# Two transformer blocks at 256 positions: the wide and the narrow products of a block in turn instead of in two runs of eight

## The chip, the cores and the metric

The kernel runs on one core of a Trainium2 chip. The metric is the device time of one execution in microseconds (us), as the median of several executions.

## What is computed

Two blocks work on x, 256 positions of 2048 features, all in float32. Each one normalises, mixes, adds, normalises, runs a gated feed-forward network of width 5632 and adds:

```python
x = first_block(x, ...)      # attention (8 differential heads, 8 sparse heads), then FFN
return second_block(x, ...)  # gated linear recurrence over 16 heads, then FFN

h = rms_norm(x, pre_mix_norm[l])
proj = h @ w_in[l]                             # first block: 2048 -> 5656 columns
x = x + rms_norm(mix @ w_out[l], post_mix_norm[l])
h = rms_norm(x, pre_ffn_norm[l])
u = causal_dwconv(h @ w_up[l], conv_w[l], conv_b[l])
gate, up = jnp.split(u, 2, axis=-1)
y = (jax.nn.gelu(gate, approximate=True) * up) @ w_down[l]
x = x + rms_norm(y, post_ffn_norm[l])
```

Nearly all work is in the products with the large weights: `w_in`, `w_out`, `w_up` and `w_down` of both blocks.

## The kernel before

**Split operands.** TensorE multiplies in a reduced float32 format (fp32r). To keep precision, each operand is the sum of a high and a low half in that format, and a product is made as three: weights high by features high, weights high by features low, weights low by features high. ACT makes the high half of a weight unit (`wh`, line 143), DVE the low half (`wl`, line 144), from the raw unit `ws` that SP's queue loads (line 125). A unit is 128 x 1024 values.

**Three kinds of product.** `wave` (lines 399, 400, 406) opens a stage: eight output blocks at once, products of 256 columns. `v_unit` (lines 421, 422, 427) has positions on partitions and weights as the moving operand, up to 512 columns. `block` (lines 359 and 364) is the one that changes. It has features on partitions: its stationary operand is a 128 x 128 piece of the weights and its moving operand is the features of all 256 positions. The feature tile holds high and low halves side by side (`src.pair`), so that one product of 512 columns makes weights-high by both halves, the *wide* product: columns 0 to 255 of the bank collect high by high, columns 256 to 511 high by low. The *narrow* product, 256 columns, adds weights-low by features-high to the second half of the bank. A block adds up 16 pieces of the features, eight from each of two weight units; what one unit serves is called a half-block here: eight wide products with `h`, then eight narrow ones with `l`. `block` is used for 24 blocks of the first block's queries and keys, 56 of the recurrence's gates, and 80 in each feed-forward stage.

**What sets the order.** Instructions are issued in the order in which the program writes them, on each engine for itself. `W.take()` hands out the halves of the current unit, and, before it does, issues the load of a unit four further on and the split of the unit two further on. `ws` has five buffers, `wh` and `wl` three each, so the split of unit i + 2 has to wait until the last product that reads unit i - 1 is done: for `wh` that is the last wide product of the half-block before, for `wl` the last narrow one. Accumulators have four banks named `mm` and some borrowed from the other four, named `bg`.

**Background work.** Everything else (attention heads, the recurrence's heads, evacuation of finished blocks, convolution, gating) is written as generators that the class `Background` holds. `bg.tick()` counts, and every fourth tick calls `step()`, which lets each generator issue its next few instructions. In the stages with heads these contain small matmuls, which go into PE's queue at that place (lines 1237, 1248, 1271 and 1285 for the recurrence). A half-block has eight ticks before the change: behind wide products 0, 1, 3, 4, 6 and 7 and behind narrow products 3 and 7; the stages before it leave the count at a multiple of four, so the steps stand behind the fifth wide product and behind the last narrow one.

Of the kernel before, what the change touches and what calls it, by code (L numbers as in the profile page):

```python
# [170 lines left out]
def two_blocks(ctx: ExitStack, tc: tile.TileContext, a: dict, out: bass.AP, dbg=None):  # L171
    nc = tc.nc
    bg = Background()
# [21 lines left out]
    def mm_ps(*cuts):  # L195

        if not mm_free.free and lend[0] and banks.free:
            t, owner = bg_ps(), banks
        else:
            while not mm_free.free:  # L200
                assert bg.tasks
                bg.step()
            t, owner = ps_mm.tile([P, 512], F32, name="mm"), mm_free
        owner.free -= 1
        if owner is banks:
            lend[0] -= 1
        views = [t[:, a:b] for a, b in cuts]
        left = [len(cuts), owner]
        for v in views:
            mm_use[id(v)] = (v, left)  # L210
        return views
# [133 lines left out]
    def need(src, k):  # L345
        while k not in src.ready:
            assert bg.tasks
            bg.step()

    def block(src):  # L350


        ps, = mm_ps((0, 2 * T))
        for k0 in range(0, KB, 8):
            h, l = W.take()
            for j in range(8):
                k = k0 + j
                need(src, k)
                nc.tensor.matmul(ps, h[:, j, :], src.pair[:, k, :, :], start=k == 0, stop=False)  # L359
                if j % 3 < 2:  # L360
                    bg.tick()
            for j in range(8):
                k = k0 + j
                nc.tensor.matmul(ps[:, T:], l[:, j, :], src.hi[:, k, :], start=False, stop=k == KB - 1)  # L364
                if j % 4 == 3:
                    bg.tick()
        return ps

    def whole(ps):
# [340 lines left out]
    with first:  # L710
# [352 lines left out]
        for i in range(8):  # L1063
            if i % 2 == 0:
                c = slice(i // 2 * CH, (i // 2 + 1) * CH)
                nc.sync.dma_start(x[:, :, c], xv[:, :, c])
            if i in (1, 4, 5):
                c = {1: 1, 4: 2, 5: 3}[i]
                later(evac_v, v_chunk(hhl, VW[c]), c)
            bg.add(start_nsa(i, block(hhl)))  # L1070
            qk = q3.tile([P, 2, T], F32, name="dqk")
            bg.add(start_diff(i, block(hhl), qk, 0))
            bg.add(start_diff(i, block(hhl), qk, 1))
# [362 lines left out]
```

## Time and profile before

| | |
|---|---|
| median of 3 runs | 2579.96 us (2578.93 to 2581.62) |
| the profiled execution | 2579.38 us |
| its span, first to last instruction | 2577.6 us |
| PE (matmul) busy | 2547.7 us, 99% |
| DVE busy | 1771.3 us, 69% |
| ACT busy | 1365.8 us, 53% |
| POOL busy | 46.5 us, 2% |
| mean granted TensorE clock | 0.999 of full speed |

Engines are PE (TensorE's matmuls), PEld (its weight loads, which overlap matmuls), DVE, ACT, POOL and SP. A row of a group of instructions gives line, engine, operation, `out<-in`, shape and count, then busy time in us and the mean duration of one in ns, then idle time before them. A matmul's duration reaches from its start to its modelled end and overlaps with the matmuls behind it, so durations don't add up to time; distances between starts do. A timeline row gives start and length in us of a run of like instructions, with the count at its end. A row on a single line in a short window gives the least, middle and largest duration of the instructions that run in that window, in ns. Blocks run from 103 to 338 us (first block's attention, with other products between), from 485 to 934 (first feed-forward stage), from 1256 to 1722 (recurrence) and from 1875 to 2324 (second feed-forward stage).

### The profile page before, as it was taken

What the parts mean: (1) busy time and instruction counts of PE and PEld (TensorE: products, weight loads), DVE (VectorE), ACT (ScalarE), POOL (GpSimd) and SP (SyncE); (2) the same over time, 40 slices, a digit from 0 to 9 for tenths busy, and PEclk for the clock granted to TensorE, in tenths of its full rate; (3) what the DMA queues carried; (4) which work ended last, traced back from release to release, by engine and by line L of the source; (5) the groups of instructions that cost most, each with busy time, mean ns of one, the idle gap of its engine ahead of it and who ended that gap; (6) DMA issues with size and microseconds to landing.
All of it is one profiled execution on the core that took longest, in us unless ns stands there. A gap on an engine that the chain in (4) does not pass through costs nothing.

```text
span 2577.6 us, 38072 instructions
## 1 busy us (share of the span) xinstructions
PE 2547.7 (99%) x14400; PEld 2223.9 (86%) x14400; DVE 1771.3 (69%) x2967; ACT 1365.8 (53%) x2274; POOL 46.5 (2%) x66
## 2 busy tenths in 40 slices
PE   9999999999999999999999999999999999999998
PEld 9899988988888888889888888888988888888887
DVE  6666655687777764446777777785678877775444
ACT  5655554665555553445555555554565555554443
POOL 0000000000000000000000000000000000000000
PEclk9999999999999999999999999999999999999999
DMA  7854555556555565555544454546556555556554
GB/s 243 263 172 148 170 172 179 173 185 192 189 189 186 192 205 188 188 188 169 165 161 158 142 170 143 166 133 196 166 175 194 189 186 192 190 188 205 188 188 147
DMA packets 134229, 466.13 MB, mean 181 GB/s; under 512 B 15547, under 2 KB 20572, under 8 KB 133532
## 3 DMA queue, kind: packets, MB, share of 16 engines
q1 hardware_dynamic: 130572, 456.11, 54.9%
q10 hardware_dynamic: 2784, 2.92, 0.6%
q0 software_dynamic: 688, 4.65, 0.5%
q8 instruction: 113, 1.85, 0.3%
q14 instruction: 72, 0.59, 0.1%
HBM read 460.74 MB, written 2.88 MB: 180 GB/s over the span
## 4 chain that ended last, share of the span: by engine, by line
PE 93%; DVE 3%; ACT 2%; issue 1%; DMA 1%; POOL 0%; DVEq 0%; POOLq 0%; ACTq 0%; SPq 0%
PE mm L359 32%; PE mm L364 17%; PE mm L422 9%; PE mm L421 9%; PE mm L427 9%; PE mm L399 2%; PE mm L400 2%; PE mm L406 2%; PE bg L1248 2%; DVE wl L144 1%; ACT wh L143 1%; PE bg L421 1%; PE bg L422 1%; PE bg L427 1%; DMA ws<-in_cw 1%
## 5 line engine op out<-in xcount | busy, mean ns | idle before, releaser
L144 DVE TENSOR_TENSOR wl<-ws,wh 128x1024 fp32r<-128x1024 f32 (+1 forms) x865 | 1049.7, 1214 | 701.4 <-ACT wh L143 693.8
L143 ACT ACTIVATE wh<-ws 128x1024 fp32r<-128x1024 f32 (+1 forms) x865 | 906.5, 1049 | 743.4 <-PE mm L422 297.5
L359 PE MATMUL mm<-hhl,wh 128*128 128x512 f32 x3808 | 982.7, 396 | 3.5 <-ACT ah L1141 3.5
L359 PEld LDWEIGHTS mm<-hhl,wh 128*128 128x128 f32 x3808 | 679.3, 189 | 120.6 <-ACT ah L1141 3.8
L364 PEld LDWEIGHTS mm<-hhl,wl 128*128 128x128 f32 x3808 | 519.2, 190 | 38.1
L364 PE MATMUL mm<-hhl,wl 128*128 128x256 f32 x3808 | 530.6, 282 | 0.0
L422 PE MATMUL mm<-wh,al 128*128 128x512 f32 x684 | 269.9, 395 | 0.0
L421 PE MATMUL mm<-wh,ah 128*128 128x512 f32 x684 | 269.9, 395 | 0.0
L427 PE MATMUL mm<-wl,ah 128*128 128x512 f32 x684 | 186.7, 395 | 0.0
L427 PEld LDWEIGHTS mm<-wl,ah 128*128 128x128 f32 x684 | 128.9, 188 | 30.1
L422 PEld LDWEIGHTS mm<-wh,al 128*128 128x128 f32 x684 | 128.9, 188 | 30.0
L421 PEld LDWEIGHTS mm<-wh,ah 128*128 128x128 f32 x684 | 128.9, 188 | 30.0
L1228 ACT ACTIVATE kk<-lv 128x256 f32<-128x256 f32 x112 | 47.7, 435 | 118.1 <-DVE lv L1259 105.2
L399 PE MATMUL mm<-hhl,wh 128*128 128x256 f32 x398 | 104.8, 295 | 4.7 <-ACT wh L143 4.7
L400 PE MATMUL mm<-hhl,wh 128*128 128x256 f32 x398 | 101.0, 285 | 0.0
L376 DVE TENSOR_TENSOR part<-mm,part 128x256 f32<-128x256 f32 x238 | 99.3, 417 | 0.0
L374 ACT ACTIVATE part<-mm 128x256 f32<-128x256 f32 x238 | 87.2, 366 | 0.2
L1116 DVE SCALAR_TENSOR_TENSOR u<-z,c_convw,u 128x256 f32<-128x256 f32 x176 | 84.8, 482 | 3.1
L1116 DVE SCALAR_TENSOR_TENSOR u<-z,c_f2conv,u 128x256 f32<-128x256 f32 x176 | 84.8, 482 | 3.1
L399 PEld LDWEIGHTS mm<-hhl,wh 128*128 128x128 f32 x398 | 77.3, 194 | 5.3 <-ACT wh L143 4.7
L1248 PE MATMUL bg<-lv,kk 128*128 128x128 f32 x448 | 74.0, 288 | 5.8 <-ACT kk L1228 5.6
L1248 PEld LDWEIGHTS bg<-lv,kk 128*128 128x128 f32 x448 | 65.0, 191 | 16.1 <-ACT kk L1228 10.3
(380 smaller groups left out, 2638.0 us busy)
## 6 DMA issues: line engine op xcount, KB each, us to landing
ws<-in_wup SPq DMA_DIRECT2D x160, 512.0 KB, 3.9
ws<-in_f2in SPq DMA_DIRECT2D x160, 512.0 KB, 3.9
ws<-in_hin SPq DMA_DIRECT2D x112, 512.0 KB, 3.5
ws<-in_wdown SPq DMA_DIRECT2D x88, 512.0 KB, 3.4
ws<-in_f2out SPq DMA_DIRECT2D x88, 512.0 KB, 3.4
ws<-in_win_f SPq DMA_DIRECT2D x48, 512.0 KB, 4.0
ws<-in_hv SPq DMA_DIRECT2D x32, 512.0 KB, 3.4
ws<-in_win_vb SPq DMA_DIRECT2D x24, 384.0 KB, 3.2
```

The source lines that it names most:

```text
L143: self.nc.scalar.activation(h[:, c], src[:, c], AF.Copy)
L144: self.nc.vector.tensor_tensor(l[:, c], src[:, c], h[:, c], op=ALU.subtract)
L359: nc.tensor.matmul(ps, h[:, j, :], src.pair[:, k, :, :], start=k == 0, stop=False)
L364: nc.tensor.matmul(ps[:, T:], l[:, j, :], src.hi[:, k, :], start=False, stop=k == KB - 1)
L376: nc.vector.tensor_tensor(s, ps[:, :T], s, op=ALU.add)
L399: nc.tensor.matmul(pss[b], h[:, b, :], src.hi[:, k, :], start=first, stop=False, skip_group_check=True)
L400: nc.tensor.matmul(pss[b], h[:, b, :], src.lo[:, k, :], start=False, stop=False, skip_group_check=True)
L421: nc.tensor.matmul(ps, rows_of(src, k0 + j, t, 0), h[:, j, :], start=k0 + j == 0, stop=False)
L422: nc.tensor.matmul(ps, rows_of(src, k0 + j, t, 1), h[:, j, :], start=False, stop=False)
L427: nc.tensor.matmul(ps, rows_of(src, k0 + j, t, 0), l[:, j, :], start=False, stop=k0 + j == last)
L1116: nc.vector.scalar_tensor_tensor(u, z[:, j:j + T], cw[:, i, j:j + 1], u, op0=ALU.mult, op1=ALU.add)
L1248: nc.tensor.matmul(ps[:, t * P:(t + 1) * P], kk[:, t * P:(t + 1) * P], view(lv, T + t * P, [[2 * m, nb], [T + m, 2], [1, m]]), start=True, ...
```

## The change

Each wide product is followed at once by the narrow one of the same piece of features, and each such pair by one tick.

```diff
                 nc.tensor.matmul(ps, h[:, j, :], src.pair[:, k, :, :], start=k == 0, stop=False)
-                if j % 3 < 2:
-                    bg.tick()
-            for j in range(8):
-                k = k0 + j
                 nc.tensor.matmul(ps[:, T:], l[:, j, :], src.hi[:, k, :], start=False, stop=k == KB - 1)
-                if j % 4 == 3:
-                    bg.tick()
+                bg.tick()
         return ps
```

A half-block still has eight ticks. The order of instructions on ACT, DVE, POOL and SP stays as it was; on PE it changes at 480 half-blocks. In the listings below a row is an instruction, or a run of like ones with its count, with the tiles that it writes and reads and what it waits for; behind line 364 the changed kernel's line numbers are four or five lower (364 becomes 360, 1248 becomes 1243).

On PE, the first step in a half-block of the recurrence's gates, before (`mm` is the block's bank, `hhl2` the features, `lv` and `kk` belong to a head of the recurrence):

```order
L359 MATMUL mm_12107<-hhl2_11235,wh_12059 128x512 x5
L1248 MATMUL bg_12121<-lv_12050,kk_12073 128x128 [waits PE_49,Activation_49]
L1248 MATMUL bg_12121<-lv_12050,kk_12073 128x128
L359 MATMUL mm_12107<-hhl2_11235,wh_12059 128x512 x3
L364 MATMUL mm_12107<-hhl2_11235,wl_12060 128x256 x8
```

The same place in the changed kernel, from the fourth pair to the fifth:

```order
L359 MATMUL mm_12107<-hhl2_11235,wh_12059 128x512
L360 MATMUL mm_12107<-hhl2_11235,wl_12060 128x256
L1243 MATMUL bg_12124<-lv_12050,kk_12073 128x128 [waits PE_49,Activation_49]
L1243 MATMUL bg_12124<-lv_12050,kk_12073 128x128
L359 MATMUL mm_12107<-hhl2_11235,wh_12059 128x512
L360 MATMUL mm_12107<-hhl2_11235,wl_12060 128x256
```

The head's two small products now stand behind four wide and four narrow products instead of five wide ones.

On PE, from one half-block of the same block into the next, before:

```order
L364 MATMUL mm_12107<-hhl2_11235,wl_12060 128x256 x8
L359 MATMUL mm_12107<-hhl2_11235,wh_12082 128x512 [waits Activation_49]
L359 MATMUL mm_12107<-hhl2_11235,wh_12082 128x512 x7
L364 MATMUL mm_12107<-hhl2_11235,wl_12083 128x256 [waits DVE_49]
L364 MATMUL mm_12107<-hhl2_11235,wl_12083 128x256 x7
```

And in the changed kernel:

```order
L359 MATMUL mm_12107<-hhl2_11235,wh_12059 128x512
L360 MATMUL mm_12107<-hhl2_11235,wl_12060 128x256
L359 MATMUL mm_12107<-hhl2_11235,wh_12082 128x512 [waits Activation_49]
L360 MATMUL mm_12107<-hhl2_11235,wl_12083 128x256 [waits DVE_49]
L359 MATMUL mm_12107<-hhl2_11235,wh_12082 128x512
```

The first product that needs `wl`, which waits for DVE, stands behind one wide product of its half-block instead of eight, and the last product that reads `wh` stands one product before the end of its half-block instead of eight.

## Rows read from the trace of the kernel before

**Rows 1.** The page, busy time and slices: engine totals, then granted clock by slice.

```profile
PE 2547.7 (99%) x14400; PEld 2223.9 (86%) x14400; DVE 1771.3 (69%) x2967; ACT 1365.8 (53%) x2274; POOL 46.5 (2%) x66
...
PEclk9999999999999999999999999999999999999999
```

**Rows 2.** The page, chain that ended last: shares of the span by line.

```profile
PE mm L359 32%; PE mm L364 17%; PE mm L422 9%; PE mm L421 9%; PE mm L427 9%; PE mm L399 2%; PE mm L400 2%; PE mm L406 2%; PE bg L1248 2%; DVE wl L144 1%; ACT wh L143 1%; PE bg L421 1%; PE bg L422 1%; PE bg L427 1%; DMA ws<-in_cw 1%
```

**Rows 3.** The page, costliest groups: the two lines of a block.

```profile
L359 PE MATMUL mm<-hhl,wh 128*128 128x512 f32 x3808 | 982.7, 396 | 3.5 <-ACT ah L1141 3.5
...
L364 PE MATMUL mm<-hhl,wl 128*128 128x256 f32 x3808 | 530.6, 282 | 0.0
```

**Rows 4.** Groups by line and shape, PE: the rest of the wide products.

```profile
L359 PE MATMUL bg<-hhl,wh 128*128 128x512 f32 x32 | 8.0, 392 | 0.0
```

**Rows 5.** Timeline of PE, 800 to 814 us: start, length, what, count.

```profile
800.01 2.00 PE L359 MATMUL mm<-hhl,wh 128*128 128x512 f32 x8
801.85 1.12 PE L364 MATMUL mm<-hhl,wl 128*128 128x256 f32 x8
802.81 2.00 PE L359 MATMUL mm<-hhl,wh 128*128 128x512 f32 x8
...
813.98 0.40 PE L359 MATMUL mm<-hhl,wh 128*128 128x512 f32 x1
```

**Rows 6.** Single lines in short windows: duration min/median/max in ns, first and last start.

```profile
L364 PE MATMUL mm<-hhl,wl x1: 277/277/277, 801.9 to 801.9; 128*128 128x256 f32 x1
...
L359 PE MATMUL mm<-hhl,wh x1: 396/396/396, 802.8 to 802.8; 128*128 128x512 f32 x1
...
L359 PE MATMUL mm<-hhl,wh x2: 389/394/398, 803.0 to 803.3; 128*128 128x512 f32 x2
...
L359 PE MATMUL mm<-hhl,wh x2: 389/392/395, 803.3 to 803.5; 128*128 128x512 f32 x2
...
L359 PE MATMUL mm<-hhl,wh x2: 389/391/393, 803.7 to 804.0; 128*128 128x512 f32 x2
...
L359 PE MATMUL mm<-hhl,wh x2: 389/389/389, 804.2 to 804.4; 128*128 128x512 f32 x2
...
L364 PE MATMUL mm<-hhl,wl x3: 277/283/283, 801.9 to 802.1; 128*128 128x256 f32 x3
```

**Rows 7.** Single lines, long windows: 512 columns twice, then 256; same columns.

```profile
L427 PE MATMUL mm<-wl,mh x47: 389/389/389, 372.7 to 419.8; 128*128 128x512 f32 x47
...
L427 PE MATMUL mm<-wl,ah x288: 390/393/404, 949.9 to 1148.6; 128*128 128x512 f32 x144
...
L406 PE MATMUL mm<-hhl,wl x76: 281/283/283, 1191.7 to 1229.0; 128*128 128x256 f32 x76
```

**Rows 8.** Waits (us in total, times, longest): stage of 500 to 930, then PE.

```profile
ACT wh L143 <- PE mm L359: 106.8, 62, 2.0
...
PE bg L1248 <- ACT kk L1228: 5.6, 8, 1.6
...
PE bg L1237 <- POOL ks L1219: 0.9, 2, 0.7
```

**Rows 9.** Timeline of all engines, 801.8 to 803.6, then 557.5 to 563.5.

```profile
801.63 0.39 PE L359 MATMUL mm<-hhl,wh 128*128 128x512 f32 x1
...
802.10 1.06 ACT L143 ACTIVATE wh<-ws 128x1024 fp32r<-128x1024 f32 x1 [0.19 <-ACT part L374]
...
803.20 1.23 DVE L144 TENSOR_TENSOR wl<-ws,wh 128x1024 fp32r<-128x1024 f32 x1 [0.72 <-ACT wh L143]
...
557.82 1.22 DVE L144 TENSOR_TENSOR wl<-ws,wh 128x1024 fp32r<-128x1024 f32 x1
...
559.79 2.00 PE L359 MATMUL mm<-hhl,wh 128*128 128x512 f32 x8
```

**Rows 10.** Timeline of PE among the second block's heads, 1380 to 1392 us.

```profile
1382.59 1.33 PE L359 MATMUL mm<-hhl,wh 128*128 128x512 f32 x5
1383.76 0.65 PE L1248 MATMUL bg<-lv,kk 128*128 128x128 f32 x4
```

## Prediction

> **What bounds the kernel now.** I read the page from the top. TensorE is busy for 99% of the span and its granted clock stays at its upper level [rows 1]; the chain of work that ended last has as its two largest entries the two lines of this change, 32% and 17% of the span [rows 2]. So the time is the sum of the distances between matmul starts, and nothing else has to be late for a nanosecond per matmul to count. The two lines make 3808 products each into the banks named mm [rows 3] and 32 more into borrowed banks [rows 4]: 3840 wide ones (512 columns), 3840 narrow ones (256 columns), 480 half-blocks of eight and eight.
>
> What one half-block costs is read from the timeline in the first feed-forward stage: the wide runs begin at 800.01 and, five half-blocks later, at 813.98 [rows 5]. That is 13.97 / 5 = 2.794 us, or 349.25 ns for a wide and narrow pair; 3840 pairs are 1341 us, half the span. The question is only whether a pair costs less or more than 349.25 ns when its members alternate.
>
> **Where inside a run the nanoseconds go.** The mean durations (396 and 282 ns) overlap and are no price. But a matmul's recorded duration follows the distance to the next start at a constant offset, so single durations show what each place in a run costs. In the half-block from 802.81 the wide products take 396, 398, 389, 395, 393, then 389 three times, and the first narrow of the run before took 277 and its later ones 283 [rows 6]. Their sum over eight and eight is 3138 + 277 + 7 x 283 = 5396 ns; less 2794 leaves 2602, so the offset is 162.6 ns for each of 16. Start to start this gives four prices:
> - wide, first after a narrow: 396 - 162.6 = 233.4 ns; wide, settled: 226.4 ns
> - narrow, first after a wide: 277 - 162.6 = 114.4 ns; narrow, settled: 120.4 ns
>
> A run of wides needs five products to come down from 233 to 226, while a narrow is cheapest directly after a wide. Long runs agree in part: 512-column products sit at 389 in one stage, but at 393 with excursions to 404 in another, and a long stream of 256-column ones sits at 283 [rows 7]. So a run has a settled pace, a disturbance costs some 7 ns a product for a few products, and there is a second, unsettled pace for wides.
>
> **The change, part by part.** *Removed or added work:* none; the same 7680 products with the same operands and as many weight loads. As the order listing shows, ACT, DVE, POOL and SP keep their order; only PE's changes.
>
> *Switches.* A half-block has one step from wide to narrow and one back; it will have eight of each. The trace of before shows no alternating stream, so each pair is bounded by the nearest rows. Lowest: every wide settled and every narrow as the first one of a run, 226.4 + 114.4 = 340.8 ns. Highest: every wide as the first one of a run and every narrow settled, 233.4 + 120.4 = 353.8 ns. Between them lie two combinations that agree: both settled, 226.4 + 120.4 = 346.8, and both as directly after a switch, 233.4 + 114.4 = 347.8. I take 346.8, because a strictly periodic stream is what settles in these rows, and the other reading lands one nanosecond away. The sum: (349.25 - 346.8) x 3840 = 9.4 us less; with 347.8 it would be 5.6 us less.
>
> As many weight loads lie under a narrow product as before (eight of sixteen), and the first narrow of a run has a full load under it too and still takes 114.4 [rows 6]: the load itself does not fix the 120.4. [...]
>
> *Release of wh.* The last wide of a half-block moves behind seven narrows, so its wh buffer comes free 7 x 120.4 = 0.84 us later. ACT's split waits for just that, 106.8 us in all in the first feed-forward stage [rows 8], so splits there start later. Typical slack: the split that starts on ACT at 802.10, right after the last wide of its predecessor, is finished by DVE at 804.43 [rows 9], and its half-block begins at 808.39, two half-blocks after 802.81 [rows 5]. Moved by 0.84 us it still leaves over 3 us. Behind a waiting split stand, on ACT, the evacuation of the block just finished and the conv steps, and on DVE the lower split; PE meets them again only when a bank comes round, and with four banks and 5.6 us for a block of two half-blocks that is far off.
>
> *Need of wl.* The first narrow moves from 1.84 us into the half-block to 0.23 us. At the typical place wl is there 4.2 us ahead, 3.3 with the later release. At the tightest place that I found in that stage, the split ends at 557.82 + 1.22 = 559.04 and the half-block begins at 559.79 [rows 9]; need moves to 560.02, slack 0.98 us, 0.14 if the split also slips by 0.84. I cost it at nothing; the cover is these two buffers of lead. Were it gone at ten such places at 0.8 us each, it would be 8 us; the rows give no sign of so many.
>
> *Background steps.* One step per four ticks, two per half-block, as before; the first moves from behind five wides (1.17 us) to behind four pairs (1.39 us) [rows 10], the second stays at the end. Where its products are at the front of PE's queue, PE has waited 5.6 + 0.9 us in all for ACT and POOL [rows 8]. Placing a step 0.22 us later gives its inputs time and delays its results by as much. Between half of these waits gone and twice as many I write -3 to +6 us and take zero.
>
> Sum: 2579.4 (the profiled execution: span 2577.6 and 1.8 us around it) - 9.4 = 2570.0 us. The median of the runs, 2579.96, is 0.6 us above that execution and changes nothing.
>
> **The rivals.**
> 1. *Every narrow is the cheap one.* If 114.4 belongs to any narrow that directly follows a wide, and the wide settles regardless, the pair is 340.8 and the time 2579.4 - 8.45 x 3.84 = 2547. For it: each first narrow that I looked at is 277. Against it: the wide behind a narrow is never settled in the rows. [...]
> 2. *No effect.* The wide stays in its unsettled stretch, at the mean of its second to fifth place, (398 + 389 + 395 + 393) / 4 - 162.6 = 231.2, and the narrow lies halfway, 117.4: 348.6 ns, 2.5 us less, 2577. The second pace in [rows 7] shows that wides can stay unsettled for hundreds of products.
> 3. *Slower.* Each wide pays the switch, 233.4, and the narrow does not get its discount because the wide before it has not settled: 120.4. The pair is 353.8, 4.55 ns more, 2579.4 + 17.5 = 2597. The point that decides is 349.25 ns per pair: with a narrow at 120.4 a wide above 228.9 makes the kernel slower, and five of the eight wides of a half-block average above that today.
>
> **How the numbers follow.** Forecast (346 to 348): 0.48. Rival 1, in whole or in part: 0.15. Rival 2: 0.14. Rival 3: 0.23, since unsettled wides are in the rows and a settled alternation is not. Predicted 2570.0; the forecast's own range is 2567 to 2575 with the small terms. The range reaches down to rival 1, 2546, and up into rival 3, to 2593; outside are some 0.05 below and 0.12 above. A measurement of this kernel can tell about 0.2% (5.2 us, 1.35 ns per pair) from no change: faster is forecast plus rival 1, 0.63; same 0.14; slower 0.23.
>
> **What the new profile would show.** Right: in the feed-forward stage ten half-blocks take 27.74 us instead of 27.94, the durations of the wide line gather at one value near 389 or 396 and those of the narrow line near 283 or 277, in opposite pairing; PE's waits stay near 7 us. Rival 1 shows 389 with 277, rival 3 396 with 283, rival 2 a spread on both. Wrong in another way: idle time of PE before either line with DVE's wl as releaser (the slack of wl misread), or more waiting for kk in the second block's heads. If pairs cost 347 and the time does not fall, the loss is in such waits.

## The result and the profile after

The changed kernel takes 2598.88 us (median of 6 runs, 2592.48 to 2599.93) against 2579.47 us for the kernel before beside it (6 runs, 2578.92 to 2581.62). The ratio is 1.0067, with a 95% interval of 1.0056 to 1.0078: slower by 0.7%. The prediction said 2570.0 us and faster, in a range of 2546 to 2593; both the sign and the range were wrong. The executions of the changed kernel fall in two groups (two near 2592.5, four from 2598.0 to 2599.9); the experiments below suggest why. The profiled execution is one of the upper group: 2597.99 us, span 2596.2 us.

The page after: engine totals, granted clock by slice, then the two lines of a block (busy us and mean ns, then idle time before them). They answer to [rows 1] and [rows 3].

```profile
PE 2563.5 (99%) x14400; PEld 2221.0 (86%) x14400; DVE 1770.8 (68%) x2967; ACT 1364.9 (53%) x2274; POOL 46.4 (2%) x66
...
PEclk9999999999999999999999999999999999999999
...
L359 PE MATMUL mm<-hhl,wh 128*128 128x512 f32 x3808 | 1366.0, 402 | 6.5 <-ACT ah L1136 4.9
...
L360 PE MATMUL mm<-hhl,wl 128*128 128x256 f32 x3808 | 1069.5, 281 | 0.0
```

TensorE is busy for 99% as before, for 2563.5 us instead of 2547.7, 15.8 us more. Most of the loss lies inside the stream of products, where no wait is recorded. The idle time before the wide line also rose, from 3.5 us [rows 3] to 6.5 us.

By stage, from the start of the first wide product of the stage's blocks to the start of its last half-block, in us (two experiments told of below stand beside the two kernels, because the comparison uses them):

| stage | before | changed | `late_start` | `one_tile` |
|---|---|---|---|---|
| first block's blocks | 232.4 | 233.2 | 233.2 | 233.2 |
| first feed-forward stage | 446.6 | 454.8 | 451.4 | 447.2 |
| recurrence | 462.4 | 464.9 | 464.9 | 465.2 |
| second feed-forward stage | 446.5 | 453.3 | 451.3 | 447.3 |
| the profiled execution | 2579.38 | 2597.99 | 2592.58 | 2584.19 |

The four stages account for 18.3 of the 18.6 us lost, 15.0 of them in the feed-forward stages.

**The pace of a pair.** Timeline of PE in the changed kernel around 800 us, the same place as [rows 5]: start, length, what.

```profile
800.10 0.40 PE L359 MATMUL mm<-hhl,wh 128*128 128x512 f32 x1
800.34 0.28 PE L360 MATMUL mm<-hhl,wl 128*128 128x256 f32 x1
800.45 0.40 PE L359 MATMUL mm<-hhl,wh 128*128 128x512 f32 x1
800.69 0.28 PE L360 MATMUL mm<-hhl,wl 128*128 128x256 f32 x1
800.81 0.40 PE L359 MATMUL mm<-hhl,wh 128*128 128x512 f32 x1
801.05 0.28 PE L360 MATMUL mm<-hhl,wl 128*128 128x256 f32 x1
801.16 0.40 PE L359 MATMUL mm<-hhl,wh 128*128 128x512 f32 x1
```

Three pairs take 801.16 - 800.10 = 1.06 us, 353.3 ns each, against 349.25 before. The single lines over 300 us of the same stage give count, least, middle and largest duration in ns, first and last start:

```profile
L359 PE MATMUL mm<-hhl,wh x850: 395/398/403, 599.8 to 899.7; 128*128 128x512 f32 x170
...
L360 PE MATMUL mm<-hhl,wl x850: 277/281/284, 600.0 to 900.0; 128*128 128x256 f32 x170
```

850 pairs in 299.9 us are 353.2 ns apart. Three pairs come round for the rest of the stage: wide 395 with narrow 281, 403 with 284, 398 with 277. By the starts the distances are some 233 and 117, 241 and 120, 236 and 113 ns, 1060 in all; each is its duration less 162 to 165 ns. The kernel before has 860 pairs in the same window:

```profile
L359 PE MATMUL mm<-hhl,wh x860: 389/389/398, 599.8 to 899.4; 128*128 128x512 f32 x172
```

In the first three half-blocks of the same stage, however, the changed kernel runs otherwise. The two lines from 486 to 491 us:

```profile
L359 PE MATMUL mm<-hhl,wh x13: 392/395/395, 485.8 to 489.9; 128*128 128x512 f32 x13
...
L360 PE MATMUL mm<-hhl,wl x13: 274/280/280, 486.0 to 490.2; 128*128 128x256 f32 x13
```

Counted from the starts there, a half-block takes 2.77 us behind the first, 346.7 ns per pair: the forecast's price, to the tenth. So the same alternation has two paces. By the starts, the change from one to the other falls in the fourth half-block of the stage, before the gap told of next.

**The start of a stage.** Between 491 and 600 us lies a gap. PE's waits (us in total, times, longest); the wait for `kk` was 5.6 before [rows 8], and the one that the profile puts down to `ah` was this:

```profile
PE mm L359 <- ACT ah L1141: 3.5, 2, 1.8
```

In the changed kernel:

```profile
PE bg L1243 <- ACT kk L1223: 6.8, 11, 1.7
PE mm L359 <- ACT ah L1136: 4.9, 2, 2.5
...
PE mm L359 <- DVE part L371: 1.6, 2, 0.8
```

The wait for `part` is new on this line. `part` is the step on DVE that ends the evacuation of a block and frees its bank. `ah` holds features that ACT makes for a later product; no block reads it, so the timeline has to show what that wait was for.

Timeline of ACT, DVE and PE around the gap, the kernel before first: the last wide products of the half-block ahead, ACT's split, its convolution step, `part`, `ah`, and the first product behind the gap; in brackets the idle time ahead and what ended it:

```profile
504.69 1.77 PE L359 MATMUL mm<-hhl,wh 128*128 128x512 f32 x7
...
506.54 1.06 ACT L143 ACTIVATE wh<-ws 128x1024 fp32r<-128x1024 f32 x1 [0.81 <-ACT wh L143]
...
507.51 0.58 ACT L1111 ACTIVATE u<-z,c_convb,c_convw 128x256 f32<-128x256 f32 x1
...
508.62 0.42 DVE L376 TENSOR_TENSOR part<-mm,part 128x256 f32<-128x256 f32 x1
...
508.73 0.42 ACT L1141 ACTIVATE ah<-u 128x256 fp32r<-128x256 f32 x1 [0.64 <-DVE u L1138]
...
509.18 2.08 PE L359 MATMUL mm<-hhl,wh 128*128 128x512 f32 x8 [1.77 <-ACT ah L1141]
```

The changed kernel, the same and the wide products behind the gap:

```profile
507.00 0.40 PE L359 MATMUL mm<-hhl,wh 128*128 128x512 f32 x1
...
507.48 1.06 ACT L143 ACTIVATE wh<-ws 128x1024 fp32r<-128x1024 f32 x1 [0.91 <-ACT wh L143]
...
508.44 0.59 ACT L1106 ACTIVATE u<-z,c_convb,c_convw 128x256 f32<-128x256 f32 x1
...
509.46 0.42 DVE L371 TENSOR_TENSOR part<-mm,part 128x256 f32<-128x256 f32 x1
...
509.57 0.42 ACT L1136 ACTIVATE ah<-u 128x256 fp32r<-128x256 f32 x1 [0.55 <-DVE u L1133]
...
510.02 0.77 PE L359 MATMUL mm<-hhl,wh 128*128 128x512 f32 x1 [2.51 <-ACT ah L1136]
...
510.80 0.63 PE L359 MATMUL mm<-hhl,wh 128*128 128x512 f32 x1
...
511.44 0.63 PE L359 MATMUL mm<-hhl,wh 128*128 128x512 f32 x1
```

In both kernels the split starts 0.08 us behind the end of the last wide product (506.46 and 507.40), which releases its buffer. It comes 0.94 us later, the convolution step behind it on ACT 0.93, `part`, behind the rest of the convolution on DVE, 0.84, and PE starts 0.84 us later: the 0.84 us by which `wh` is released later, passed on in full.

PE starts 0.14 us behind the end of `part` in both kernels (509.04 and 509.88). It does so within 0.01 us at each of these waits, also where no `ah` ends near it, as at the new waits. So what the profile calls a wait for `ah` is a wait for a bank; `ah` and `part` stand behind the same step on DVE and so end together. Behind the gap a pair takes 511.44 - 510.80 = 0.64 us instead of 0.35. Table by stretch: length, busy us and count of PE, PEld, DVE, ACT and POOL, then the granted clock, the DMA share and GB/s:

```profile
492.00:507.00 15.00, 15.00 (x87) 12.83 (x85) 11.15 (x19) 9.79 (x15) 0.00 (x0) 1.00 0.49 164
...
509.50:512.70 3.20, 2.68 (x8) 2.32 (x9) 3.13 (x7) 1.29 (x3) 0.00 (x0) 0.52 0.51 150
513.00:520.00 7.00, 6.19 (x35) 5.15 (x35) 4.33 (x7) 3.49 (x6) 0.00 (x0) 1.00 0.40 140
```

The granted clock was 0.52 of full speed in these 3.2 us, and 0.50 from 509.90 to 512.80 us. From the starts, the eighth to tenth half-blocks of the stage take 5.49 + 4.25 + 3.80 = 13.54 us, before 4.73 + 2.87 + 2.97 = 10.57. In the second feed-forward stage they go from 10.47 to 12.10, at a granted clock of 1.00 (1904 to 1915 us). There the eighth half-block is 0.78 us longer and the tenth 0.84: the old wait for a bank, lengthened, and the new one. The late split delays the evacuation behind it, and PE meets it at the bank.

### The profile page after: what moved, and what is told of

Read it like the earlier page. It is cut to its first block, busy times and chain, and to the rows that moved or that the text cites. A ratio compares the mean times of both kernels' runs of the same rounds, so it can differ in the third digit from the quotient of the medians.

```text
span 2596.2 us, 38072 instructions
## 1 busy us (share of the span) xinstructions
PE 2563.5 (99%) x14400; PEld 2221.0 (86%) x14400; DVE 1770.8 (68%) x2967; ACT 1364.9 (53%) x2274; POOL 46.4 (2%) x66
## 3 DMA queue, kind: packets, MB, share of 16 engines
HBM read 460.74 MB, written 2.88 MB: 179 GB/s over the span
## 4 chain that ended last, share of the span: by engine, by line
PE 92%; DVE 4%; ACT 2%; issue 1%; DMA 1%; POOL 0%; DVEq 0%; POOLq 0%; ACTq 0%; SPq 0%
PE mm L359 32%; PE mm L360 16%; PE mm L416 9%; PE mm L417 9%; PE mm L422 9%; PE mm L394 2%; PE mm L395 2%; PE mm L401 2%; PE bg L1243 2%; DVE wl L144 1%; ACT wh L143 1%; PE bg L416 1%; PE bg L417 1%; PE bg L422 1%; DMA ws<-in_cw 1%
## 5 line engine op out<-in xcount | busy, mean ns | idle before, releaser
L359 PE MATMUL mm<-hhl,wh 128*128 128x512 f32 x3808 | 1366.0, 402 | 6.5 <-ACT ah L1136 4.9
L360 PE MATMUL mm<-hhl,wl 128*128 128x256 f32 x3808 | 1069.5, 281 | 0.0
L359 PEld LDWEIGHTS mm<-hhl,wh 128*128 128x128 f32 x3808 | 716.7, 188 | 178.4 <-ACT ah L1136 5.5
L360 PEld LDWEIGHTS mm<-hhl,wl 128*128 128x128 f32 x3808 | 720.5, 189 | 0.2
L394 PEld LDWEIGHTS mm<-hhl,wh 128*128 128x128 f32 x398 | 77.2, 194 | 5.3 <-ACT wh L143 4.6
L416 PE MATMUL mm<-wh,hhl 128*128 128x512 f32 (+1 forms) x208 | 78.0, 375 | 0.0
```

Of the source, the lines that this page charges most:

```text
L394: nc.tensor.matmul(pss[b], h[:, b, :], src.hi[:, k, :], start=first, stop=False, skip_group_check=True)
L416: nc.tensor.matmul(ps, rows_of(src, k0 + j, t, 0), h[:, j, :], start=k0 + j == 0, stop=False)
```

## The experiments

The theories under test: **PACE**, the settled pair costs 353.3 ns and that is the loss; **RELEASE**, the later release of `wh` makes PE wait at the start of a stage. Later, when the two paces had been seen, came theories on what selects the pace: **BANK** (which half of a bank the narrow product adds to), **LOADS** (reading weights from two tiles in turn), **START** (how the stream is entered) and **DRIFT** (the slow pace is where the stream goes whatever the start). Edits are shown against the changed kernel, those of `late_wh` and `late_start` against the kernel before. Where several kernels ran together they share the runs of the kernel before (2579.9 to 2580.1 us).

### The changed kernel again

> The changed kernel once more, unaltered, because its six times lie in two groups (2592.5 twice, 2598 to 2600 four times). Two theories are on the table. PACE: in a long alternation a wide and a narrow product together take 353.3 ns instead of 349.2, 16 us over 3840 pairs. RELEASE: the wh buffer comes free 0.84 us later, the evacuations behind ACT's waiting split are late, PE stands idle at the start of the feed-forward stages (2.5 us where it was 1.8), and what follows runs at a lower clock; some 3 us per feed-forward stage. PACE expects the groups to differ in the pace of some stage (346.7 ns in 1280 pairs of one feed-forward stage would be 8.5 us less); RELEASE expects them to differ in the stretch after the idle time (1 to 3 us each). Both: 2592 to 2600.

Measured: 2598.62 us (2590.01 to 2601.46), ratio 1.0063 (1.0049 to 1.0077). From the thirteenth on, half-blocks average 2.827 us in both feed-forward stages of the profiled execution (2601.46 us). The first result stands, the spread of its times too.

### One size: groups of four and of two

```diff
-            for j in range(8):
-                k = k0 + j
-                need(src, k)
-                nc.tensor.matmul(ps, h[:, j, :], src.pair[:, k, :, :], start=k == 0, stop=False)
-                nc.tensor.matmul(ps[:, T:], l[:, j, :], src.hi[:, k, :], start=False, stop=k == KB - 1)
-                bg.tick()
+            for j0 in range(0, 8, 4):      # 2 in groups_of_2
+                for j in range(j0, j0 + 4):
...
+                for j in range(j0, j0 + 4):
...
```

> Four wide, four narrow, twice per half-block. PACE, by the prices of the first four places of a run: 233.4 + 235.4 + 226.4 + 232.4 for the wides, 114.4 + 120.4 x 3 for the narrows, 351 ns per pair, 1.8 more than before, 7 us: 2584 to 2588; a locked pace of its own could give anything between 2570 and 2596. RELEASE: wh is released half as late (0.48 us), so about half of the idle time that was added, 1 us per feed-forward stage: 2580 to 2582.

> Two wide, two narrow, four times per half-block. PACE by the prices of the first two places of a run: 233.4 + 235.4 and 114.4 + 120.4, 351.8 per pair, 2.6 more than before, 10 us, and 1 to 3 us for a release of wh 0.24 us later: 2590 to 2593. A locked pattern of its own may lie elsewhere: a settled multiple of 6.67 ns per group, 693.3 (346.7 per pair) would give 2571 to 2573, 706.7 (353.3) 2596 to 2599.

Measured: groups of four 2588.41 us, ratio 1.0032 (1.0019 to 1.0044); groups of two 2584.44 us over 10 runs, 1.0014 (1.0005 to 1.0023). The single line over 600 to 900 us, four and then two:

```profile
L360 PE MATMUL mm<-hhl,wh x856: 387/396/398, 599.7 to 899.3; 128*128 128x512 f32 x172
```

```profile
L360 PE MATMUL mm<-hhl,wh x862: 393/396/398, 599.8 to 899.8; 128*128 128x512 f32 x173
```

From the starts, a pair costs 350.8 ns in fours and 348.3 in twos, against 349.2 in eights and 353.3 in ones. The price doesn't rise or fall steadily with the number of switches: "each switch costs" and "each switch pays" both fall. Groups of two have the better pace and still lose. PE's waits for a bank that the profile puts down to `ah`, in groups of four and then of two:

```profile
PE mm L360 <- ACT ah L1139: 4.3, 2, 2.2
```

```profile
PE mm L360 <- ACT ah L1139: 4.9, 2, 2.5
```

Behind the last wide product of a half-block four narrow ones fewer follow in fours and six fewer in twos, which delays the release by 0.48 and 0.72 us, an estimate at the settled 0.12 us of a narrow product (not by the 0.24 that the expectation for twos took), against 0.84 in the changed kernel. The longest wait goes with it: 1.8 us before, then 2.2, 2.5 and 2.5. The time of groups of two lies outside all ranges that were expected. PACE alone doesn't explain it; RELEASE, at 0.72 us and with the lower clock behind the gap (0.85 of full speed in 507 to 514 us and 0.76 in 1904 to 1911; the ninth half-block takes 4.34 and 4.41 us in the two stages, before 2.87 and 2.88), does.

### The release alone: all narrow products but one ahead of the last wide one

```diff
-            for j in range(8):
+            for j in range(7):
...
+            for j in range(8):
+                k = k0 + j
+                if j == 7:
+                    need(src, k)
+                    nc.tensor.matmul(ps, h[:, j, :], src.pair[:, k, :, :], start=False, stop=False)
+                    bg.tick()
                 nc.tensor.matmul(ps[:, T:], l[:, j, :], src.hi[:, k, :], start=False, stop=k == KB - 1)
```

> Seven wide, seven narrow, then the last wide and the last narrow product of each half-block: the wh buffer is released as late as in the changed kernel, but nearly all products stay in runs. PACE: two switches per half-block more than before, worth between 1 and 7 ns each half, so 2579 to 2583, and the idle time at the start of the feed-forward stages near 1.8 us. RELEASE: the idle time of 2.5 us and the low clock behind it come back, 3 us per feed-forward stage: 2584 to 2588.

Measured: 2590.48 us (2590.06 to 2593.41), ratio 1.0042 (1.0029 to 1.0055). PE's waits, then the gap in the timeline, then the stretch around it:

```profile
PE mm L359 <- ACT ah L1145: 5.0, 2, 2.6
```

```profile
511.16 1.85 PE L359 MATMUL mm<-hhl,wh 128*128 128x512 f32 x7 [2.57 <-ACT ah L1145]
```

```profile
507.00:514.00 7.00, 4.43 (x27) 3.73 (x26) 6.00 (x12) 3.54 (x6) 0.00 (x0) 1.00 0.49 158
```

Runs of seven, with one wide and one narrow product behind them, are all but the order before, and the longer wait is there in full: the release makes it. But the granted clock stayed at 1.00 behind 2.57 us of idle, so the length of the gap alone doesn't bring the lower one. The edit isn't as clean as meant: two more switches make a half-block 2.807 us, 13 ns more, or 6.4 us over 480. The rest, some 4 us, is RELEASE; with both, the time lies above either expectation.

### The start in runs, the rest in turn

```diff
-    def block(src):
+    def block(src, paired=True):
...
-                bg.add((up_task if i % 2 else gate_task)(i, block(hhl)))
+                bg.add((up_task if i % 2 else gate_task)(i, block(hhl, i >= WAVE + 8)))
```

With `paired` false the block runs as in the kernel before: the first eight blocks of each feed-forward stage.

> The changed kernel, but the first eight blocks of each feed-forward stage keep runs of eight, so that the stretch in which PE stood idle passes before the alternation begins; the other 72 blocks (144 half-blocks) alternate. RELEASE: the idle time at the start of a stage goes back to 1.8 us and no stretch at half clock follows, 2 to 4 us less than the changed kernel per stage. PACE: what the 72 blocks cost hangs on the pattern that they fall into, 346.7 or 353.3 ns per pair, both of which the changed kernel's trace shows (its first three half-blocks of a stage take 2.77 us each, later ones 2.83). Both stages at 353.3: 2580 + 9.6 + 5 for the other blocks = 2594; both at 346.7: 2580 - 5.8 + 5 = 2579; one of each 2587.

Measured: 2592.03 us (2591.28 to 2592.60), ratio 1.0043 (1.0030 to 1.0055). PE's waits, then the single line over 300 us:

```profile
PE mm L359 <- ACT ah L1143: 3.5, 2, 1.8
```

```profile
L359 PE MATMUL mm<-hhl,wh x850: 395/398/403, 599.8 to 899.8; 128*128 128x512 f32 x170
```

The wait is back to 3.5 us, longest 1.8, as before, and the two groups of times are gone. What is left is the pace: the feed-forward stages are 4.8 us longer than before each (table above), and 144 half-blocks by 33 ns are 4.8. So the changed kernel's 15.0 us there are some 9.6 PACE and 5.4 what happens at the start. Of those 5.4, PE's waits for banks are 3.0 (4.9 - 3.5 + 1.6) and the lower clock some 1.4 (an estimate: the ninth half-block of the first stage, 4.25 - 2.87); the last us isn't traced.

### What selects the pace: bank and weights

In `psum_first` the narrow product adds to the first half of the bank, which gives the same sum in the end; in `one_tile` it reads the high half of the weights again, so that the product of the weights' low half is left out.

```diff
-                nc.tensor.matmul(ps[:, T:], l[:, j, :], src.hi[:, k, :], start=False, stop=k == KB - 1)
+                nc.tensor.matmul(ps[:, :T], l[:, j, :], src.hi[:, k, :], start=False, stop=k == KB - 1)   # psum_first
+                nc.tensor.matmul(ps[:, T:], h[:, j, :], src.hi[:, k, :], start=False, stop=k == KB - 1)   # one_tile
```

> The changed order, with the narrow product added to the first half of the bank, which the wide product in front of it wrote 227 ns earlier, instead of to the second, written 120 ns earlier; the two halves are added up afterwards, so the result is the same. A theory BANK: the narrow product has to wait for the columns that the wide one has just written; then the pace falls below 349 and the time to 2580 or less, but for the idle time. PACE (where starts fall, not what is written): 346.7 or 353.3 per pair as before, 2590 to 2601.

> The changed order, with the narrow product's weights taken from the high half too: the product with the low half of the weights is left out, and PE never waits for wl in the blocks. A theory LOADS: weights that come from two tiles in turn, or the wait for DVE's half, make the pair dear; then the pace falls to 347 or less throughout and the idle time at the stage's start shrinks: 2575 to 2585. PACE and RELEASE: wh is still released by the last product, the idle time stays at 2.5 us and the pair at 353.3 (or 346.7 in one stage): 2590 to 2601.

Measured: `psum_first` 2595.88 us (2589.68 to 2601.16), ratio 1.0064 (1.0049 to 1.0080); `one_tile` 2595.12 us (2584.19 to 2602.70), 1.0054 (1.0035 to 1.0074). The medians say little; single lines say more. The wide line of `psum_first` in the first and in the second feed-forward stage of one execution (2589.68 us):

```profile
L359 PE MATMUL mm<-hhl,wh x867: 391/391/391, 599.6 to 899.9; 128*128 128x512 f32 x174
...
L359 PE MATMUL mm<-hhl,wh x850: 395/398/403, 1999.9 to 2299.9; 128*128 128x512 f32 x170
```

The same of `one_tile`, in the execution of 2584.19 us:

```profile
L359 PE MATMUL mm<-hhl,wh x866: 391/391/391, 599.9 to 899.7; 128*128 128x512 f32 x174
...
L359 PE MATMUL mm<-hhl,wh x867: 391/391/391, 1999.7 to 2299.9; 128*128 128x512 f32 x174
```

BANK and LOADS fall: the same code takes either pace in different stages of one execution, and holds it for hundreds of pairs. No trace shows when the columns of a bank are written: the 227 and 120 ns of the first expectation are an estimate, near the settled distances of 512 and 256 columns, 226.4 and 120.4 ns. A stage of some 148 half-blocks is 148 x 53 ns = 7.9 us longer at 353.3 than at 346.7. That fits the distance between the groups of times, and the four profiled executions of these three orders lie where it says: 2584.19 us with both stages fast, 2589.68 with one, 2597.99 and 2601.46 with none. The six times of `one_tile` then show all three groups; those of the changed kernel, by their distance, the upper two. That its lower group had a fast stage is not shown, since both of its profiled executions settled slow. The gap takes part in the choice: up to it the three stages that settled at 346.7 ns a pair, too, ran at 2.83 us a half-block, and all three had a lower clock behind it (0.76, 0.76 and 0.87 of full speed over 7 us there), as had three of the five that settled at 353.3 (0.76, 0.77 and 0.90; the other two 1.00).

The stage table adds the main point: with both stages at the forecast's pace, `one_tile` still takes 447.2 and 447.3 us there, 0.6 and 0.8 more than the kernel before. The gain of pace, 148 x 20 ns = 3 us a stage, goes into the start of the stage, whose wait is as long as in the changed kernel:

```profile
PE mm L359 <- ACT ah L1136: 5.2, 2, 2.6
```

### Trying to enter the fast pace

In `late_start`, one block between the runs and the alternation was written in groups of two (`hinge_2`), in groups of four (`hinge_4`), or with narrow ahead of wide in its second half-block (`hinge_nw`):

```diff
...
+            elif mode in (2, 4):
+                seq = [(s, j) for j0 in range(0, 8, mode) for s in (0, 1) for j in range(j0, j0 + mode)]
+            elif mode == 3:
+                seq = [(s, j) for j in range(8) for s in ((0, 1) if k0 == 0 else (1, 0))]
...
+                bg.add((up_task if i % 2 else gate_task)(i, block(hhl, 0 if i < WAVE + 8 else 2 if i == WAVE + 8 else 1)))
```

> As late_start (first eight blocks of a feed-forward stage in runs, 71 of the other 72 alternating), but the ninth block, the hinge, goes in groups of two, so that the alternation is entered from another pattern. If the price of a pair is only a matter of the pattern that the alternation falls into (PACE with two settled patterns, 346.7 and 353.3 ns), the stages take either 353.3 throughout, 2592 as late_start, or 346.7 throughout, 142 half-blocks x 53 ns x 2 = 15 us less, 2577, or one of each, 2584; nothing between. If 353.3 is the price of alternation as such and 346.7 was left over from a disturbed start, the time stays at 2592.

> As hinge_2 with the ninth block in groups of four. Two settled patterns: 2592, 2584 or 2577 and nothing between. One price of alternation: 2592.

> As hinge_2, but the ninth block alternates too, with the narrow product first in its second half-block, which puts two narrow products in a row at its middle and two wide ones at its end. Two settled patterns: 2592, 2584 or 2577 and nothing between. One price of alternation: 2592.

Measured: 2594.19, 2594.25 and 2591.36 us, ratios 1.0055 (1.0040 to 1.0070), 1.0055 (1.0040 to 1.0070) and 1.0046 (1.0030 to 1.0063). All six feed-forward stages of their profiled executions settled at the slow pace: both of `hinge_2` have wide durations of 395, 398 and 403 ns, and the mean of the wide line is 401 ns in all three executions.

Then `late_start` with 17 pushes in each feed-forward stage: ahead of every fourth block a small extra product whose length n grows from 72 to 88 columns in the first stage and from 96 to 112 in the second. It is added work, and its result is overwritten.

```diff
...
+        if kick:
+            nc.tensor.matmul(ps[:, :kick], ident, x[:, 0, :kick], start=True, stop=True)
```

> late_start with 17 small pushes in each feed-forward stage: before every fourth block, from the 21st on, one extra product of the identity with n columns of x in full float32, into the block's own bank, where the first wide product overwrites it; n is 72 to 88 in the first stage and 96 to 112 in the second, so that the next wide product starts at 34 different offsets. What each costs by itself, 0.1 to 0.25 us, is not the point (3 to 9 us in all). Theory START: which of the two patterns an alternation settles in is decided by the offset at which it is entered. Then the stretches between two pushes, 64 pairs each, take either 22.19 us (346.7 ns) or 22.61 us (353.3 ns) per 64 pairs, both occur, and the mean of the stages falls. Theory DRIFT: without idle time or a change of clock, every alternation ends at 353.3: all stretches take 22.61 us, and the time is 2592 plus the pushes, 2595 to 2601.

Measured: 2599.57 us (2 runs), ratio 1.0078 (1.0049 to 1.0107), the 34 pushes included: 7.5 us above `late_start`, some 0.22 a push. Of the 34 stretches of the profiled execution two ran at 346.7 ns a pair, behind n = 75 and n = 76; n = 77 ended it. The wide line behind these three pushes:

```profile
L373 PE MATMUL mm<-hhl,wh x41: 391/391/391, 631.9 to 645.8; 128*128 128x512 f32 x41
...
L373 PE MATMUL mm<-hhl,wh x47: 392/392/395, 649.8 to 665.8; 128*128 128x512 f32 x47
...
L373 PE MATMUL mm<-hhl,wh x52: 395/398/403, 671.9 to 690.0; 128*128 128x512 f32 x52
```

So a disturbance can select the pace in either direction (START), but nearly every one leads to the slow pace. DRIFT as it was worded, the slow pace always, falls with these two stretches and with the three fast stages above. How to hold the fast one on purpose stays open.

### Fewer switches: runs of sixteen

The other direction: the second half-block of a block runs narrow first, so that runs of one kind are 16 long and there is one switch per half-block instead of two.

```diff
...
+            for half in ((0, 1) if k0 == 0 else (1, 0)):
+                for j in range(8):
...
+                    if half:
+                        nc.tensor.matmul(ps[:, T:], l[:, j, :], src.hi[:, k, :], start=False, stop=False)
...
+                    else:
+                        nc.tensor.matmul(ps, h[:, j, :], src.pair[:, k, :, :], start=k == 0, stop=end)
```

> Runs of sixteen: the second half-block of each block makes its eight narrow products first and its eight wide ones after them, so that a block has one switch each way instead of two. PACE: a switch into wides costs 26 ns over the settled pace, one into narrows gives 6 back, so 20 ns less per block, 240 blocks, 4.8 us: 2574 to 2576. RELEASE: wh is released 0.96 us later in every second half-block and wl is needed at its start; half of the loss of the changed kernel's starts, 3 us, against the gain: 2577 to 2580.

Measured: 2576.37 us over 11 runs (2575.74 to 2577.52), ratio 0.9985 (0.9976 to 0.9994): faster than both kernels. Timeline of PE at 800 us, and PE's waits:

```profile
802.45 3.82 PE L366 MATMUL mm<-hhl,wh 128*128 128x512 f32 x16
806.11 2.08 PE L362 MATMUL mm<-hhl,wl 128*128 128x256 f32 x16
808.02 3.82 PE L366 MATMUL mm<-hhl,wh 128*128 128x512 f32 x16
```

```profile
PE mm L366 <- ACT u L1113: 1.8, 1, 1.8
PE mm L366 <- DVE part L378: 1.7, 1, 1.7
```

Two half-blocks take 808.02 - 802.45 = 5.57 us, 2.785 each, against 2.794; the longest wait is 1.8 us, as before, one in each feed-forward stage; with no `ah` near, the profile puts the second down to `part`. Longer runs pay the unsettled products of [rows 6] once instead of twice per two half-blocks. The gain, 3.7 us, lies below the 0.2% that the prediction called a difference, but its 95% interval lies wholly below 1.

## Why the prediction was wrong

**Switches: the price was mis-sized.** The working had its bounds right, 340.8 to 353.8 ns a pair, and took 346.8 "because a strictly periodic stream is what settles". The stream does settle, and 346.7 is one of the paces it settles at. But it has two, and it takes 353.3 in five of the eight profiled feed-forward stages that alternate from their start and behind 32 of 34 pushes, within half a nanosecond of the third rival's 353.8. The step that failed is the inference from "periodic" to "the settled price of each member". Even at the fast pace the members don't have those prices: by the starts of `one_tile` a wide is at 230 ns and a narrow at 117, where the forecast had 226.4 and 120.4 or 233.4 and 114.4. That the sum agrees to the tenth is luck. The rows of before held a warning that got only 0.14 (rival 2) and 0.23 (rival 3): 512-column products ran at 389 in one stage and at 390 to 404 for hundreds of products in another [rows 7], so one stream could have two lasting paces. The point that decides, 349.25 ns, was the right price of the old order, but it doesn't decide alone: groups of two, at 348.3, and `one_tile`, at 346.7, lie below it and are slower than the kernel before. The third rival had the time (2597 against 2597.99) in part by luck. At 353.3 the pace would cost (353.3 - 349.25) x 3840 = 15.6 us; the feed-forward stages show 9.6, and the first block and the recurrence, whose other products break the stream, lost 0.8 and 2.5 in all, some 1.2 of the latter in longer waits for `kk`. The starts of the stages, which this rival didn't have, bring the rest. Nor did its prices hold, 233.4 and 120.4 (durations of 396 and 283): the wides average 236.4 ns, dearer than a switch, and the narrows 117.0, half-way to their discount.

The working's remark that the load does not fix the price of a narrow product held: in the changed kernel, 600 to 900 us, the loads take 187 to 190 ns each, and narrows stand at 113, 117 and 120 ns in one cycle.

**Release of wh: costed at nothing, worth some 5 us.** The slack of over 3 us was read in the middle of a stage (802 us, [rows 9]). At the start of a feed-forward stage there is none: 3.5 us of idle time in front of this very line stood in [rows 3], a wait of 1.8 and one of 1.7 us, put down to `ah` but ended by `part`. The program evacuates the eight outputs of `wave` one after another over the first blocks of a stage, so that banks are short there, and ACT's split stands ahead of what frees one. The prediction named that queue ("behind a waiting split stand, on ACT, the evacuation of the block just finished and the conv steps") and the place where PE would meet it, "only when a bank comes round". The step that failed is "that is far off", judged by a typical place: in each feed-forward stage PE met it twice, for 0.74 us more in the old wait and for 0.81 in the new one. The lower clock behind the longer gap adds some 1.4 us in the first stage; no row of before showed it.

**What held.** *Need of wl:* PE's largest waits name no `wl` for the wide or the narrow line, and idle time before the narrow line is 0.0. *Background steps:* waiting for `kk` went from 5.6 to 6.8 us, inside the -3 to +6 given. *Removed or added work:* none; DVE and ACT busy times differ by under 1 us. Nor was it the *new wait* that the text feared last, idle time released by `wl`.

**Had the pace been right,** the time would most likely still not have fallen: the execution of `one_tile` at 346.7 ns a pair is 2584.19 us. It loses 0.6 and 0.8 us in the feed-forward stages, where the start eats the forecast's gain, and the rest elsewhere. That execution leaves one product's weights out and releases `wh` and `wl` otherwise, so it is a near relative and not the changed kernel itself. The fast stage of `psum_first`, which releases both as the changed kernel does, says the same: 447.3 us by the measure of the stage table, against 446.6 before.

## What to carry to other kernels

When an engine is busy for 99%, cost a reordering by the pace of the new order, and don't build that pace from the settled rows of the old one: a stream can settle at more than one, so measure it, and take the dearer combination as likely until then. Cost a later release where the wait already stands, at the front of the line that idles now, and not at a typical place. When a wait is put down to a step whose result the waiter doesn't read, compare ends and starts in the timeline. When runs of one kernel fall in groups, compare single lines between stages of one execution: that told two paces apart where the medians could not.

## What the hardware showed that was not expected

- **Two lasting paces of one order of instructions.** Alternating 512 and 256 columns, reduced float32, settles at 346.7 or 353.3 ns a pair, the second in a cycle of three pairs (1060 ns), for hundreds of pairs. The first has two patterns: wides at 391 ns throughout, or at 392 and 395 in turn as in the first half-blocks of a stage. In one execution a push of 75 columns moved it to the fast one, and a push of 77 back.
- **A pair's price by group size** is 353.3 ns in ones, 348.3 in twos, 350.8 in fours, 349.2 in eights, and 348 in sixteens (2.785 us / 8). From the thirteenth half-block of a feed-forward stage on, the mean half-block takes 2773.3 ns (ones, fast), 2786.7 (twos), 2793.3 (eights), 2806.7 (fours) and 2826.7 (ones, slow): steps of 2, 1, 2 and 3 times 6.67 ns (an eighth of 2826.7 - 2773.3). What makes these values is open.
- **Wide products came below the settled price of the working,** 226.4 ns: the shortest of a block, in groups of four, have a duration of 387 ns, which less 162.6 is some 224 ns, at a granted clock of 1.00.
- **The clock fell behind one gap and not behind a like one:** 0.52 of full speed in 509.50 to 512.70 us behind 2.51 us of idle in the changed kernel, 1.00 behind 2.57 us in `late_wh`. In both, PE's waits from 484 to 530 us are this gap and one of 0.8 us; what decided is open.
